# RWKV-7 layer with gated conv FFN: the Gram products of a head pair over 64 array rows each

## The chip, the cores and the metric

The kernel runs on one core of a Trainium2 chip. The metric is the device time of one execution in microseconds (us), the median of several runs.

## The reference, cut to what matters

One layer on x of 2048 tokens x 1024 channels, float32. The part concerned is the recurrence of 16 heads, each with a 64x64 state, between the projections and the output projection; a gated FFN with a causal convolution follows.

```python
def step(state, inp):                      # per head, token after token
    r_t, w_t, k_t, v_t, kk_t, a_t = inp
    sa = jnp.einsum('bhij,bhj->bhi', state, -kk_t)
    state = (state * w_t[:, :, None, :]
             + sa[..., None] * (kk_t * a_t)[:, :, None, :]
             + v_t[..., None] * k_t[:, :, None, :])
    return state, jnp.einsum('bhij,bhj->bhi', state, r_t)
...
mixed = ((y + bonus) * gate) @ w_o
x = _layer_norm(ALPHA * x + mixed, ln1_g, ln1_b)
x = _layer_norm(ALPHA * x + _conv_ffn(x, ...), ln2_g, ln2_b)
```

## The kernel before, in words

The program has four parts that overlap: projections and LoRAs (`a_nodes`), the recurrence (`s_nodes`), the output projection with its LayerNorm (`w_nodes`) and the FFN (`f_nodes`). Each adds groups of instructions to a planner (`Plan`). A group has an engine, an assumed duration, a due time and buffers of pools that it takes and gives back; the planner simulates the engines by these durations, and the order that comes out is the order in which each engine, and SP's queue of DMAs, gets its instructions. At run time an engine goes through its instructions in that order; one that waits holds all behind it.

The recurrence works on 16 tiles of 128 tokens, each of two chunks c of 64 tokens. Eight heads form a half h, so that a tile has two halves; a half has four pairs p of heads e = 0, 1. The step of 64 tokens is done as matrix products, for which the kernel needs, per head and chunk, all products between the decayed vectors: b (kk * a) and k on one side, the two vectors AR (-kk and r) on the other. These are the Gram products G. Per half:

- SP loads `l` (128 tokens x 5 x 512, 1280 KB) into the only buffer of the pool `lds`. csI (TensorE) is the running sum of the log decays, and P, Pe and Pi (ScalarE, L833) are its exponentials.
- VectorE multiplies two of the five parts of l by Pe and P (L851, L855); TensorE transposes them (tr, L878) and P (pcp, L864), ScalarE copies the former into AR.
- BKn (VectorE, L904) are b and k divided by the decay, for both chunks. b of head e lies in partitions 64e to 64e+63 and k in the other 64, so the two heads of a pair are stacked the opposite way, and each of the eight instructions takes four heads of one kind, 64x256. The last of them gives back the load buffer, and SP issues the next load.
- TensorE transposes BKn (tb, L912, rows are now channels: 64 of head 0, 64 of head 1). ScalarE copies head 0's rows into one tile and head 1's into another (BKT), whose other 64 rows were set to zero by POOL at the start. There is one such pair of tiles. G (TensorE, L744 called from f_g) is then a product over 128 rows for each head, four to a group, of which 64 rows are zeros. VectorE multiplies it by a mask (Gm, L931).

Per tile: parts of Gm go to DRAM and back transposed (NU, NUs); VectorE inverts 32 triangles of 32x32 in 31 steps of two instructions (itmp L966, XU L971); the result goes through DRAM again (XD, XT); X11 (L1000) transposes two blocks on VectorE, and two sets of small products (mp) complete the inverse of 64x64. Then the two chunks go one after the other: Z, SA, dS and Y on TensorE, copies on ScalarE (the state, later SA, into UV beside the values loaded by UV<-vc, and the decayed keys of AR into Gm), and on VectorE stmp (L1117) and state (L1122). The opposite stacking of the heads holds for UV and for all of these copies.

L744 is the helper for the products and L743 that for ScalarE's copies, so rows of these lines are told apart by the tile's name. The pools' sizes stand in `TS` (L730): one load buffer `lds`, four PSUM banks `pw` for csI, pcp, tr, tb and G, one `BKT`.

## Time and profile before

| | us |
|---|---|
| median of 3 runs | 2982.55 |
| lowest and highest | 2982.29 to 2985.43 |
| span of the profiled execution | 2981.2 |
| busy in it: TensorE | 2845.6 (95%) |
| VectorE | 2084.5 (70%) |
| ScalarE | 1740.4 (58%) |

The shares are means over parts with different limits. The projections end at about 735 us, the recurrence runs from about 690 to 1290 us, and the FFN fills TensorE to the end. A windows row gives the busy time of each engine in a stretch of 25 us, then the granted clock of TensorE (1.00 is 2.4 GHz, 0.50 is 1.2 GHz), DMA's share and GB/s. A chain row is a piece of the chain of work that ended last. Of overlapping instructions a row of the timeline shows the start of the first and the time to the end of the last.

### The profile page before, as it was taken

To read this page: it belongs to the slowest core of one execution; us is meant where nothing else is said; L and a number is where in the kernel's file an instruction comes from. 1 tells how busy PE (TensorE), PEld (TensorE's weight loads), DVE (VectorE), ACT (ScalarE), POOL (GpSimd) and SP (SyncE) were. 2 spreads that over 40 slices of the span, in tenths; PEclk is the share of its full clock that TensorE was granted. 3 is DMA by queue.
4 is the path that set the end of the run, shared out by engine and by line. 5 is a ranking of instruction groups with operands and counts; after the bars stand their busy time and mean duration, and the time that the engine had idled before them with its cause. 6 is when DMAs were issued, how large, how long until landed. Compare 5 with 4: busy or idle time off the path is not lost.

```text
span 2981.2 us, 51766 instructions
## 1 busy us (share of the span) xinstructions
PE 2845.6 (95%) x19392; PEld 2321.1 (78%) x19392; DVE 2084.5 (70%) x4288; ACT 1740.4 (58%) x4668; POOL 53.6 (2%) x96
## 2 busy tenths in 40 slices
PE   7999999998799999799999999999999999999997
PEld 5776778887677777678888887888888888888886
DVE  7888768986899999779765555474554745547454
ACT  8888557664578788878454444444444444444441
POOL 0000000001000000001100000000000000000000
PEclk9999999999899999799999999999999999999999
DMA  6346555435455565568552223242232422324222
GB/s 202 143 167 222 175 183 191 152 114 175 129 149 161 153 164 160 133 220 315 179 178 94 92 97 120 93 154 97 89 127 96 148 98 85 133 95 153 90 87 78
DMA packets 298555, 424.08 MB, mean 142 GB/s; under 512 B 153952, under 2 KB 179552, under 8 KB 294208
## 3 DMA queue, kind: packets, MB, share of 16 engines
q1 hardware_dynamic: 286976, 379.87, 39.5%
q0 software_dynamic: 11328, 40.90, 3.8%
q8 instruction: 153, 2.51, 0.4%
q14 instruction: 98, 0.80, 0.1%
HBM read 311.57 MB, written 109.12 MB: 141 GB/s over the span
## 4 chain that ended last, share of the span: by engine, by line
issue 56%; PE 20%; DVE 12%; ACT 8%; DMA 3%; POOL 1%; SPq 0%; POOLq 0%; ACTq 0%; DVEq 0%
PE ps L141 4%; PE ps L142 4%; PE ps L143 4%; DVE BKn L904 3%; ACT junk L619 3%; PE G L744 2%; DVE itmp L966 1%; DVE XU L971 1%; DVE Gm L931 1%; PE Y L744 1%; DMA l<-in 1%; ACT junk L1260 1%; PE csI L744 1%; ACT UV L743 1%; PE tb L912 1%
## 5 line engine op out<-in xcount | busy, mean ns | idle before, releaser
L143 PE MATMUL ps<-xH,wiL 128*128 128x512 f32 x1408 | 557.9, 396 | 0.5 <-DVE wiL L1571 0.3
L1571 DVE TENSOR_TENSOR wiL<-wis,wiH 128x1024 fp32r<-128x1024 f32 x176 | 215.4, 1224 | 488.5 <-ACT wiH L1432 488.5
L141 PE MATMUL ps<-xH,wiH 128*128 128x512 f32 x1408 | 556.9, 396 | 0.0
L142 PE MATMUL ps<-xL,wiH 128*128 128x512 f32 x1408 | 556.8, 395 | 0.0
L1432 ACT ACTIVATE hb<-ps 128x512 f32<-128x512 f32 x176 | 105.3, 598 | 518.9 <-PE ps L143 518.8
L141 PE MATMUL ps<-WH,xiH 128*128 128x512 f32 x768 | 307.5, 400 | 14.6 <-ACT xiH L231 9.1
L143 PEld LDWEIGHTS ps<-xH,wiL 128*128 128x128 f32 x1408 | 264.5, 188 | 65.6 <-DVE wiL L1571 2.1
L142 PEld LDWEIGHTS ps<-xL,wiH 128*128 128x128 f32 x1408 | 264.4, 188 | 63.7
L141 PEld LDWEIGHTS ps<-xH,wiH 128*128 128x128 f32 x1408 | 264.5, 188 | 62.9
L142 PE MATMUL ps<-WL,xiH 128*128 128x512 f32 x768 | 305.1, 397 | 2.0 <-DVE WL L326 2.0
L143 PE MATMUL ps<-WH,xiL 128*128 128x512 f32 x768 | 304.4, 396 | 0.0
L1599 DVE SCALAR_TENSOR_TENSOR cv<-hb,cw,cv 128x512 f32<-128x512 f32 x352 | 263.4, 748 | 20.7 <-ACT cv L1595 14.5
L142 PE MATMUL acc<-woL,aH 128*128 128x512 f32 x688 | 269.3, 391 | 1.5 <-DVE woL L1536 1.5
L143 PE MATMUL acc<-woH,aL 128*128 128x512 f32 x688 | 269.9, 392 | 0.0
L141 PE MATMUL acc<-woH,aH 128*128 128x512 f32 x688 | 268.5, 390 | 0.0
L1432 ACT ACTIVATE wiH<-wis 128x1024 fp32r<-128x1024 f32 x178 | 188.8, 1061 | 5.8 <-DMA wis<-in_w_in_dram 5.8
L141 PEld LDWEIGHTS ps<-WH,xiH 128*128 128x128 f32 x768 | 146.3, 190 | 54.4 <-ACT xiH L231 9.1
L1432 ACT ACTIVATE woH<-wos 128x512 fp32r<-128x512 f32 x172 | 108.7, 633 | 114.4 <-PE acc L143 110.1
L142 PEld LDWEIGHTS ps<-WL,xiH 128*128 128x128 f32 x768 | 146.5, 191 | 34.6 <-DVE WL L326 2.5
L143 PEld LDWEIGHTS ps<-WH,xiL 128*128 128x128 f32 x768 | 146.3, 190 | 33.5 <-DVE xiL L450 0.2
L142 PEld LDWEIGHTS acc<-woL,aH 128*128 128x128 f32 x688 | 129.2, 188 | 32.4 <-DVE woL L1536 3.1
L141 PEld LDWEIGHTS acc<-woH,aH 128*128 128x128 f32 x688 | 129.2, 188 | 29.1 <-ACT woH L1432 0.5
(243 smaller groups left out, 5351.8 us busy)
## 6 DMA issues: line engine op xcount, KB each, us to landing
wis<-in_w_in_dram SPq DMA_DIRECT2D x176, 512.0 KB
wos<-in_w_out_dram SPq DMA_DIRECT2D x172, 256.0 KB
l<-in SPq DMA_DIRECT2D x32, 1280.0 KB
xT<-in_xT_dram SPq DMA_DIRECT2D x21, 1028.0 KB
in<-kp SPq DMA_DIRECT2D x64, 256.0 KB
stg<-in_w_rkv_dram SPq DMA_DIRECT2D x48, 256.0 KB
gs<-gs SPq DMA_DIRECT2D x24, 512.0 KB
in<-kr SPq DMA_DIRECT2D x32, 256.0 KB
```

Of the source, the lines that this page charges most:

```text
L141: nc.tensor.matmul(ps, lH, rH, start=start, stop=False)
L142: nc.tensor.matmul(ps, lH, rL, start=False, stop=False)
L143: nc.tensor.matmul(ps, lL, rH, start=False, stop=stop)
L619: nc.scalar.activation(junk, Z["kr"][:, 64 * i:64 * i + 64], AF.Square, accum_out=st["ss"][:, tl, i:i + 1])
L743: CP = lambda out, in_, **kw: nc.scalar.activation(out, in_, AF.Copy, **kw)
L744: MM = lambda out, l, r, **kw: nc.tensor.matmul(out, l, r, **{**dict(start=True, stop=True), **kw}, skip_group_check=True)
L904: TT(dst[rows, :, e], pe8(l[:, 1 if part else 3], e), pe8(V[t]["Pi", h], e), op=OP.mult)
L912: nc.tensor.transpose(ps[:, p], V[t]["BKn"][:, c, hd:hd + 2].rearrange("q e i -> q (e i)"), self.ident)
L931: TT(V[t]["Gm"][:, e, c, 4 * h:4 * h + 4], V[t]["G", h, c, e], gm4, op=OP.mult)
L1432: CP = lambda out, in_, **kw: nc.scalar.activation(out, in_, AF.Copy, **kw)
L1571: TT(W["L"], W["s"], W["H"], op=OP.subtract)
L1599: STT(R[j], W["hb"][:, i:i + 512], C["cw"][:, fc, i:i + 1], R[j], op0=OP.mult, op1=OP.add)
```

## The change

Both heads of a pair now have b in partitions 0 to 63 and k in 64 to 127.

- BKn: one instruction takes eight heads of a kind and chunk, 64x512; four instead of eight per half. The planner's duration for a group goes from 0.67 to 0.6.
- BKT: tb is copied as it is, one 128x512 instead of two 64x512, into one of two buffers; the zeroed tiles are gone.
- G: a product takes 64 rows of the array, those where its head's channels are, and the two heads alternate, each into its own PSUM bank. Both banks are taken at once; the planner's duration is 1.05 for the eight, before 0.87 for each four.
- Gm, UV, X11 and the copies into them follow: the first 64 partitions are b's, the state's and SA's for both heads, the others k's and the values'. UV is loaded in two DMAs with 4 KB a row instead of four with 256 B pieces. NU reads partitions 0 to 63 for both heads. X11 is 32 partitions with both heads in them, and the mp products that read it use array rows 0 to 31 for both heads.

```diff
-              slots=dict(lds=1, pw=4, P=1, Pi=1, Pe=1, AR=4, BKn=4, Gm=4, PC=4, BKT=1, NUs=2, XU=2, XT0=1, XT1=1, X11=2, mp=1,
+              slots=dict(lds=1, pw=4, P=1, Pi=1, Pe=1, AR=4, BKn=4, Gm=4, PC=4, BKT=2, NUs=2, XU=2, XT0=1, XT1=1, X11=2, mp=1,
...
-            for i in range(sl["BKT"]):
-                BKTs.append([wkp.tile([128, 4, 128], F32, name=f"BKT{i}{e}") for e in range(2)])
...
-        def f_zero1():
-            for x in BKTs:
-                for e in range(2):
-                    nc.gpsimd.memset(x[e], 0.0)
...
                         def f_bk(t=t, h=h, c=c, part=part):
                             l = V[t][f"l{h}"]
-                            pe8 = lambda ap, e: ap[es(c)].rearrange("t (p e i) -> t p e i", e=2, i=64)[:, :, e]
-                            dst = eo(V[t]["BKn"][:, c, 8 * h:8 * h + 8])
-                            for e in range(2):
-                                rows = es(1 - e) if part else es(e)
-                                TT(dst[rows, :, e], pe8(l[:, 1 if part else 3], e), pe8(V[t]["Pi", h], e), op=OP.mult)
+                            dst = V[t]["BKn"][es(part), c, 8 * h:8 * h + 8].rearrange("t h i -> t (h i)")
+                            TT(dst, l[es(c), 1 if part else 3], V[t]["Pi", h][es(c)], op=OP.mult)
                         last = c == 1 and part == 1
-                        n_bks.append(pl.add("DVE", 0.67, hb + 1.1 + c, f_bk, [n_Pi, n_alloc, n_R, n_M] +
+                        n_bks.append(pl.add("DVE", 0.6, hb + 1.1 + c, f_bk, [n_Pi, n_alloc, n_R, n_M] +
...
                     def f_bt(t=t, h=h, c=c):
-                        x = V[t]["BKT", h, c] = BKTs[st_bkt[0] % len(BKTs)]
-                        st_bkt[0] += 1
-                        for e in range(2):
-                            CP(x[e][es(e)], V[t]["tb", h, c][es(e)])
+                        CP(tile_of(t, ("BKT", h, c), wkp, [128, 4, 128], tag="BKT", bufs=sl["BKT"]), V[t]["tb", h, c])
-                    n_bt = pl.add("ACT", 0.96, hb + 2.1 + c, f_bt, [n_tb, n_z1], take=("BKT",), give=("pw",))
+                    n_bt = pl.add("ACT", 0.6, hb + 2.1 + c, f_bt, [n_tb], take=("BKT",), give=("pw",))
...
+                    def f_g(t=t, h=h, c=c):
+                        G = [tile_of(t, ("G", h, c, e), pw, [128, 4, 128], tag="pw") for e in range(2)]
+                        for p in range(4):
+                            for e in range(2):
+                                MM(G[e][:, p], V[t]["BKT", h, c][es(e), p],
+                                   V[t]["AR"][es(e), c, 4 * h + p].rearrange("q a t -> q (a t)"))
+                    n_g = pl.add("PE", 1.05, hb + 2.2 + c, f_g, [n_bt] + evs, take=("pw", "pw"), give=("BKT",))
                     for e in range(2):
-                        def f_g(t=t, h=h, c=c, e=e):
-                            G = tile_of(t, ("G", h, c, e), pw, [128, 4, 128], tag="pw")
-                            for p in range(4):
-                                MM(G[:, p], V[t]["BKT", h, c][e][:, p],
-                                   V[t]["AR"][:, c, 4 * h + p].rearrange("q a t -> q (a t)"))
-
...
-                        n_g = pl.add("PE", 0.87, hb + 2.2 + c + 0.1 * e, f_g, [n_bt] + evs + gs, take=("pw",),
-                                     give=("BKT",) if e else ())
-                        gs.append(n_g)
...
-                        r, u = 64 * e + 32 * bk, (e * 2 + bk) * 16
+                        r, u = 32 * bk, (e * 2 + bk) * 16
...
-                    x = tile_of(t, ("X11", c), wk, [128, 8, 32], tag="X11", bufs=sl["X11"])
+                    x = tile_of(t, ("X11", c), wk, [32, 2, 8, 32], tag="X11", bufs=sl["X11"])
                     for e in range(2):
-                        nc.vector.transpose(x[es(e)], XT[es(e), :, 0:32])
+                        nc.vector.transpose(x[:, e], XT[64 * e:64 * e + 32, :, 0:32])
...
-                            MM(mp[r + 32:r + 64, p], V[t]["Gm"][r:r + 32, e, c, p, 32:64], V[t]["X11", c][r:r + 32, p],
-                               tile_position=(r, r + 32))
+                            MM(mp[r + 32:r + 64, p], V[t]["Gm"][0:32, e, c, p, 32:64], V[t]["X11", c][:, e, p],
+                               tile_position=(0, r + 32))
...
-                        CP(V[t]["Gm"][es(e), e, c, :, 0:64], V[t]["AR"][es(e), c, :, 0])
+                        CP(V[t]["Gm"][0:64, e, c, :, 0:64], V[t]["AR"][es(e), c, :, 0])
...
                 for c in range(2):
-                    src = self.S["vc", t][64 * c:64 * c + 64].rearrange("t (p e i) -> t p e i", e=2, i=64)
-                    for e in range(2):
-                        self.ld(eo(UV[:, c])[es(1 - e), :, e], src[:, :, e])
+                    self.ld(UV[64:128, c].rearrange("t h i -> t (h i)"), self.S["vc", t][64 * c:64 * c + 64])
...
-                            CP(eo(V[t]["UV"][:, c])[es(e), sl8, e], SV[i0][es(e), sl8])
+                            CP(eo(V[t]["UV"][:, c])[0:64, sl8, e], SV[i0][es(e), sl8])
...
-                            CP(eo(V[t]["UV"][:, c])[es(e), sl8, e], H["SA"][es(e), sl8])
+                            CP(eo(V[t]["UV"][:, c])[0:64, sl8, e], H["SA"][es(e), sl8])
```

The planner's result changes with it. VectorE in the first half of a tile in the steady part of the recurrence, before; l is the half's load, BKn, itmp and XU as above (itmp and XU belong to the inverse of another tile):

```order
L966 TENSOR_TENSOR itmp<-XU,NUs 128x121
L904 TENSOR_TENSOR BKn<-l_12705,Pi 64x4x64 x2
L971 TENSOR_TENSOR XU<-XU,itmp 128x11x11
L904 TENSOR_TENSOR BKn<-l_12705,Pi 64x4x64 x2
L966 TENSOR_TENSOR itmp<-XU,NUs 128x110
L904 TENSOR_TENSOR BKn<-l_12705,Pi 64x4x64 x2
L971 TENSOR_TENSOR XU<-XU,itmp 128x11x10
L904 TENSOR_TENSOR BKn<-l_12705,Pi 64x4x64 x2
L966 TENSOR_TENSOR itmp<-XU,NUs 128x108
```

The same place on VectorE now:

```order
L949 TENSOR_TENSOR itmp<-XU,NUs 128x121
L891 TENSOR_TENSOR BKn<-l_12600,Pi 64x512
L954 TENSOR_TENSOR XU<-XU,itmp 128x11x11
L891 TENSOR_TENSOR BKn<-l_12600,Pi 64x512
L949 TENSOR_TENSOR itmp<-XU,NUs 128x110
L1098 TENSOR_TENSOR stmp<-dS,state 128x512
L954 TENSOR_TENSOR XU<-XU,itmp 128x11x10
L1103 TENSOR_TENSOR state<-stmp,PC 128x512
L949 TENSOR_TENSOR itmp<-XU,NUs 128x108
L891 TENSOR_TENSOR BKn<-l_12600,Pi 64x512
L954 TENSOR_TENSOR XU<-XU,itmp 128x12x9
L891 TENSOR_TENSOR BKn<-l_12600,Pi 64x512
```

stmp and state, which stood behind the half's last BKn, now stand between its two chunks.

TensorE at the second half of a tile in the steady part, before (csI to tb are the half's, SA, dS and Y another tile's chunk step):

```order
L744 MATMUL csI<-l_9669,c_triI 128x512
L744 MATMUL G<-AR,BKT_7382 128x128 x4
L744 MATMUL SA<-Zs,XT_7829 64x64 x16
L864 MATMUL pcp<-ident,P 128x128 x4
L878 MATMUL tr<-ident,l_9669 128x128 x8
L744 MATMUL dS<-UV,BKn 64x64 x16
L912 MATMUL tb<-ident,BKn 128x128 x8
L744 MATMUL G<-AR,BKT_7381 128x128 x4
L744 MATMUL Y_9767<-UV,Gm 64x64 x16
L744 MATMUL G<-AR,BKT_7382 128x128 x4
```

TensorE at the second half of a tile now:

```order
L744 MATMUL G<-AR,BKT 128x128 x8
L744 MATMUL SA<-Zs,XT_7822 64x64 x16
L744 MATMUL csI<-l_10745,c_triI 128x512
L744 MATMUL dS<-UV,BKn 64x64 x16
L854 MATMUL pcp<-ident,P 128x128 x4
L868 MATMUL tr<-ident,l_10745 128x128 x8
L899 MATMUL tb<-ident,BKn 128x128 x8
L744 MATMUL G<-AR,BKT 128x128 x16
```

G now stands in eights and sixteens and SA ahead of csI, and dS has moved from behind tr to directly behind csI.

## Rows read from the trace of the kernel before

**Rows 1.** Table of windows: PE, PEld, DVE, ACT, POOL busy us, clock, DMA

```profile
750.00:775.00 25.00, 18.42 (x95) 15.35 (x95) 20.56 (x71) 9.38 (x19) 0.00 (x0) 0.73 0.49 146
...
800.00:825.00 25.00, 19.96 (x310) 16.45 (x311) 23.50 (x81) 14.87 (x29) 0.54 (x1) 1.00 0.58 169
...
1050.00:1075.00 25.00, 22.42 (x425) 19.35 (x420) 24.18 (x82) 20.02 (x42) 0.00 (x0) 1.00 0.48 127
1075.00:1100.00 25.00, 23.92 (x472) 20.35 (x471) 23.98 (x82) 21.95 (x44) 0.53 (x1) 1.00 0.61 168
```

**Rows 2.** List of waits, 875 to 1200 us: total, times, longest

```profile
PE csI L744 <- DMA l<-in: 1.3, 3, 0.6
...
DVE l L855 <- ACT P L833: 0.6, 1, 0.6
```

**Rows 3.** Groups of VectorE by form, 875 to 1200 us

```profile
L904 DVE TENSOR_TENSOR BKn<-l,Pi 64x256 f32<-64x256 f32 x166 | 68.6, 418 | 3.1 <-ACT Pi L833 0.3
...
L855 DVE TENSOR_TENSOR l<-l,P 128x512 f32<-128x512 f32 x21 | 14.4, 684 | 0.6 <-ACT P L833 0.6
```

**Rows 4.** Chain of waits, 719 to 727 us: start, us, what

```profile
719.34 6.20 DMA l<-in
725.58 1.14 PE csI L744 x2
```

**Rows 5.** Timeline of TensorE, 750 to 757 us: start, us, what

```profile
750.00 5.46 PE L744 MATMUL G<-AR,BKT 128*128 128x128 f32 x32
755.30 1.02 PE L744 MATMUL csI<-l,c_triI 128*128 128x512 f32 x2
```

**Rows 6.** Timeline of VectorE, second half of a tile, 1099 to 1104 us

```profile
1099.85 2.50 DVE L904 TENSOR_TENSOR BKn<-l,Pi 64x256 f32<-64x256 f32 x6
1102.38 0.27 DVE L971 TENSOR_TENSOR XU<-XU,itmp 128x110 f32<-128x110 f32 x1
1102.68 0.86 DVE L904 TENSOR_TENSOR BKn<-l,Pi 64x256 f32<-64x256 f32 x2
1103.57 0.29 DVE L966 TENSOR_TENSOR itmp<-XU,NUs 128x126 f32<-128x126 f32 x1
```

**Rows 7.** Timeline of VectorE, 1066 to 1068 us

```profile
1066.22 0.68 DVE L855 TENSOR_TENSOR l<-l,P 128x512 f32<-128x512 f32 x1
1066.82 0.68 DVE L931 TENSOR_TENSOR Gm<-G,c_gmask 128x512 f32<-128x512 f32 x1
```

**Rows 8.** Timeline of TensorE, 1064 to 1067 us

```profile
1064.67 1.05 PE L744 MATMUL G<-AR,BKT 128*128 128x128 f32 x8
1065.65 1.15 PE L744 MATMUL SA<-Zs,XT 64*64 64x64 f32 x32
1066.73 0.66 PE L864 MATMUL pcp<-ident,P 128*128 128x128 f32 x4
```

**Rows 9.** List of waits, 690 to 875 us

```profile
ACT BKT L743 <- PE G L744: 17.0, 10, 2.8
...
DVE Gm L931 <- PE G L744: 14.1, 13, 3.6
```

**Rows 10.** Groups of ScalarE by form, 875 to 1200 us

```profile
L743 ACT ACTIVATE BKT<-tb 64x512 f32<-64x512 f32 x81 | 47.9, 592 | 11.8 <-PE tb L912 10.3
...
L743 ACT ACTIVATE Zs<-Z 128x512 f32<-128x512 f32 x18 | 10.7, 597 | 0.2
```

**Rows 11.** Timeline of SP's queue, 1011 to 1014 us

```profile
1011.27 2.59 SPq L124 DMA_DIRECT2D UV<-vc  x4
```

**Rows 12.** Chain of waits, at the last tile

```profile
1210.40 3.52 DMA NU<-Gm
```

**Rows 13.** Chain of waits, a load of the steady part

```profile
1008.51 8.39 DMA l<-in
```

**Rows 14.** Chain of waits, G at the low and at the high clock

```profile
765.70 3.43 PE G L744 x16
...
1058.67 1.98 PE G L744 x16
```

More of the change, by code (lines that the diff above doesn't have):

```diff
@@ L746, in s_nodes @@
         es = lambda e: slice(64 * e, 64 * e + 64)
-        st_bkt = [0]
         eo = lambda tl: tl.rearrange("q (p e) i -> q p e i", e=2)
@@ L800, in s_nodes @@
         cst = wk = ch2 = sm = pm = pc = None
-        chs, XTs, BKTs, SV, ZS, SW, V = [None] * sl["AR"], [], [], {}, {}, {}, {}
+        chs, XTs, SV, ZS, SW, V = [None] * sl["AR"], [], {}, {}, {}, {}
         n_o1 = pl.add("-", 0, 0, f_open1, [n_1])
         n_o2 = pl.add("-", 0, 0, f_open2, [n_o1, n_2])
-        n_z1 = pl.add("POOL", 2.0, -9.0, f_zero1, [n_o1], lat=0.2)
         n_z2 = pl.add("POOL", 4.0, -9.0, f_zero2, [n_o2], lat=0.2)
@@ L915, in f_bt @@
                     def f_bt(t=t, h=h, c=c):
-                        x = V[t]["BKT", h, c] = BKTs[st_bkt[0] % len(BKTs)]
-                        st_bkt[0] += 1
-                        for e in range(2):
-                            CP(x[e][es(e)], V[t]["tb", h, c][es(e)])
+                        CP(tile_of(t, ("BKT", h, c), wkp, [128, 4, 128], tag="BKT", bufs=sl["BKT"]), V[t]["tb", h, c])
                     n_tb = pl.add("PE", 0.44, hb + 2.0 + c, f_tb, n_bks[2 * c:2 * c + 2], take=("pw",))
-                    n_bt = pl.add("ACT", 0.96, hb + 2.1 + c, f_bt, [n_tb, n_z1], take=("BKT",), give=("pw",))
-                    gs = []
-                    for e in range(2):
-                        def f_g(t=t, h=h, c=c, e=e):
-                            G = tile_of(t, ("G", h, c, e), pw, [128, 4, 128], tag="pw")
-                            for p in range(4):
-                                MM(G[:, p], V[t]["BKT", h, c][e][:, p],
-                                   V[t]["AR"][:, c, 4 * h + p].rearrange("q a t -> q (a t)"))
+                    n_bt = pl.add("ACT", 0.6, hb + 2.1 + c, f_bt, [n_tb], take=("BKT",), give=("pw",))
[6 more added lines that the diff above has]
+                    n_g = pl.add("PE", 1.05, hb + 2.2 + c, f_g, [n_bt] + evs, take=("pw", "pw"), give=("BKT",))
+                    for e in range(2):
                         def f_gm(t=t, h=h, c=c, e=e):
                             TT(V[t]["Gm"][:, e, c, 4 * h:4 * h + 4], V[t]["G", h, c, e], gm4, op=OP.mult)
-                        n_g = pl.add("PE", 0.87, hb + 2.2 + c + 0.1 * e, f_g, [n_bt] + evs + gs, take=("pw",),
-                                     give=("BKT",) if e else ())
-                        gs.append(n_g)
                         grams.append(pl.add("DVE", 0.6, hb + 2.3 + c + 0.1 * e, f_gm, [n_g], give=("pw",)))
```

## The prediction

> **What bounds the kernel now.** I read the table of windows first. In the steady part of the recurrence (about 800 to 1201 us) VectorE is busy 24.18 and 23.98 of 25 us, while TensorE has 22.42 and 23.92 and ScalarE 20.02 and 21.95 [rows 1]. VectorE is full there: in the list of waits of 875 to 1200 us the longest wait of VectorE for another engine is 0.6 us, and TensorE waited for the load of the recurrence's inputs 1.3 us in all [rows 2]. So a time taken off VectorE is a time taken off that stretch, until something else is late. The stretch's pace comes from the grouped instructions: 166 BKn of 8 per half tile are 20.75 halves in 325 us, 15.66 us a half and 31.3 us a tile [rows 3].
>
> Before 800 us it is another limit. At 750 to 775 us no engine is full (TensorE 18.42, VectorE 20.56) and the granted clock is 0.73 [rows 1]. The chain there runs in a ring: load, csI, P, the decayed l, BKn, and the next load, since there is one load buffer and the last BKn gives it back. One such ring shows in the chain of waits: the load takes 6.20 us and csI starts 0.04 us behind it [rows 4]. TensorE goes its queue in order, so csI can also stand behind the G products: 32 records of G take 5.46 us at this clock and csI starts right behind them [rows 5]. After 1201 us the last tiles' latency counts, then the FFN, whose work is untouched.
>
> **The sum.** It is made against the profiled span of 2981.2 us; the median of the runs, 2982.55 us, lies 1.35 us above it, and I carry that difference over.
>
> *BKn, 8 of 64x256 to 4 of 64x512 per half.* The timeline shows 8 BKn with one XU between them from 1099.85 to 1103.57, 3.72 us; the XU takes 0.30 of it (1102.38 to 1102.68), so 3.42 us, 0.43 each, which is the record's 418 ns and 0.01 [rows 3, 6]. No 64x512 of VectorE is in the trace. The nearest row is the 128x512 product l·P, with the same number of elements in a partition: a record of 684 ns [rows 3], whose successor starts 0.60 us after it [rows 7]. The new one costs 0.60 us if its successor starts as early, and 0.70 if it starts after the record's end, as behind the BKn of now. Four are 2.40 to 2.80 us, so a half saves 0.62 to 1.02 us. The operands still alternate between the lower and upper 64 partitions, as now, so I stay near 0.70 and take 0.65.
>
> The Trainium skill, page "VectorE: DVE Perf Modes", section "Two Vector instructions with no wait between them", says that an instruction whose inputs or output begin in another quadrant than those of the one ahead starts only when all earlier ones have finished. The rows agree: 0.60 us between two 128x512 that start alike, 0.43 us for a 418 ns record that doesn't. By that rule alone three or four of each four new BKn cost 0.70, and the sum below would be 2961 rather than 2960.
>
> The last 24 of the 32 halves lie in the full stretch (400 us at 15.66, less the cut one): 24 x 0.65 = 15.6 us. Seven halves lie on the ring of 700 to 800 us, where the last BKn releases the load: 7 x 0.65 = 4.6 us. The first half lies beside the projections.
>
> *G over 64 rows.* Each product is two records. Four G products with 128 columns take 0.98 us (1064.67 to 1065.65), 0.245 each; SA, 16 products of 64 columns that alternate between two quarters of the array, takes 1.08 (to 1066.73), 0.0675 each [rows 8]. At G's rate 64 columns would take 0.122; so SA runs 1.8 abreast. A tile has 32 G products, 7.8 us; at 1.8 they are 4.3. TensorE's load per tile, 46.34/50 x 31.3 = 29.0 us [rows 1], falls to 25.5. In the steady stretch that is hidden behind VectorE and counts nothing. On the ring it counts where csI or the mask Gm wait for G: VectorE waited 14.1 us for G in 690 to 875 us, ScalarE's BKT copy 17.0 us for G, for want of a second BKT [rows 9]. Both buffers and products now come sooner, but csI is then held by the load (6.20 us from the last BKn is about where csI starts now). The gain is between 0 and 14.1 us; I take 0.4 us a half, 3 us, because the ring row shows only 0.04 us between load and csI.
>
> *BKT, one copy for two.* Two of 592 ns become one of 128x512, like Zs at 597 ns [rows 10]: 64 x 0.59 = 38 us off ScalarE, hidden, as VectorE hardly waits for ScalarE [rows 2]. The zeroing on POOL was off the path.
>
> *Moved rows.* The copies of decayed keys, state and SA into rows 0 to 63 keep their shapes; X11 becomes 32x256 and keeps its elements in a partition. The mp products of both heads share 32 array rows now in other columns; dS and Z share rows in this way already and are as fast as SA, so nothing. UV goes in two issues instead of the four that take 2.59 us on SP's queue [rows 11], ahead of NU and of the next load: at best 1.3 us earlier for what is queued behind, on a stretch where loads are seldom late. NU reads 64 partitions for both heads. This is covered while VectorE has other inverses to do; at the end, where the last NU stands on the chain with 3.52 us [rows 12], it costs between 0 and once more that. I take 1 us.
>
> The Trainium skill, page "SBUF — State Buffer", section "Door 1: The DMA port swizzle", speaks against this part: partitions of one half reach only 8 of 16 ports. By it the tail's NU could double, 3.5 us, and the sum would be 2963. No row here shows such a load.
>
> Sum: 2982.5 - 15.6 - 4.6 - 3 + 1 = **2960 us**.
>
> **Rivals.** (a) *More comes back.* New BKn overlap fully (0.60): 31 halves x 1.02 = 31.6 us, and the ring gives 7 us: 2944 us. For it: the 128x512 pitch [rows 7]. Against: today's BKn don't overlap [rows 6].
>
> (b) *The row halves don't run side by side.* No product over 64 rows and 128 columns is in the trace; only quarters and column halves are. Then TensorE keeps 29.0 us for a tile that should take 30.0, 97%, where its fullest window now has 23.92 of 25 [rows 1], 96%. About half of the steady gain is lost, and the 3 us: 2982.5 - 7.8 - 4.6 = 2970 us. The Trainium skill, page "TensorEngine Tiling (Array Packing)", section "Key Properties", says that a change of tiling mode drains TensorE, which would add to this case; in the trace G and SA follow one another at their usual pitch [rows 8].
>
> (c) *A wait takes the freed place.* The planner now puts dS behind csI, and stmp, which reads dS, between the two BKn pairs of a half. A load that lands late, as that of 1008.51 with 8.39 us against 6.20 [rows 4, 13], then holds csI, dS, stmp, and behind stmp the two BKn that free the load buffer. If this costs 1.3 us a tile the steady gain is gone and the ring's is partly: 2978 to 2982 us. Against: csI waited for loads only 1.3 us in 325 [rows 2], and two UV issues burden the queues less.
>
> (d) *Slower: TensorE's clock falls in the steady stretch.* With 25.5 us of work in 30.0 TensorE has idle time that it hasn't now. 16 records of G take 3.43 us at the low level (1.2 GHz) and 1.98 at the high one (2.4 GHz) [rows 14], 1.73 times as long. A tile of 25.5 us lasts over 31.3 once a third of its work runs low: 25.5 x (1 + 0.73 s) > 31.3 from s = 0.31. At s = 0.5 it is 34.8, 3.5 us more over 12.8 tiles (400 us), 45 us; less the ring's 7, 3020 us. For it: at 750 to 775 us the granted clock was 0.73 with 18.42 busy. Against: at 800 to 825 us it stayed 1.00 with 19.96 of 25, 80%, less than the 85% to come [rows 1]. The Trainium skill, page "TensorE: Matmul & The Clock Gate", section "Why this matters for your kernels", warns of idle gaps between bursts, which is this rival's reason.
>
> **How the numbers follow.** Chances: forecast 0.57 (2950 to 2968), (a) 0.10, (b) 0.16, (c) 0.08, (d) 0.09. The forecast's own range comes from 0.62 to 1.02 us a half, 0 to 7 on the ring and 0 to 3.5 at the tail. The range of 8 in 10 takes in (a) and (b): 2944 to 2976 us. Faster by over 0.2% (6 us, about what a measurement of this kernel can tell from no change) are forecast, (a) and (b): 0.83; same is (c), 0.08; slower is (d), 0.09.
>
> **What would show it.** Right: 4 BKn of some 684 ns a half and a tile of about 30 us between 875 and 1150 us with VectorE still at 96%; G records 16 in about 1.1 us; a BKT copy of 0.6 us; granted clock 1.00. Wrong: VectorE below 93% there, with stmp waiting for dS or Gm for G (c, b); G 16 in 2 us (b); granted clock under 1.00 in the steady windows (d); ring halves at 15 us as now; a tail longer than now between the last Gm and the first FFN product, for which I have 1 us.

## The result and the profile after

The changed kernel takes 2998.67 us (median; 2995.38 to 3005.86) beside 2982.92 us for the kernel before on the same chip: ratio 1.0052, 95% interval 1.0036 to 1.0068. It is slower, where 2960 us was forecast. The profiled span is 2993.6 us, 12.4 more than before. By the end of each half's last BKn and of the last Y:

| stretch | before | after | difference |
|---|---|---|---|
| to the end of the 2nd half | 719.3 | 716.6 | -2.7 |
| 3rd to 10th half (the ring) | 129.9 | 128.0 | -1.9 |
| 11th to 28th half (nine steady tiles) | 286.2 | 296.7 | **+10.5** |
| 29th to 32nd half | 65.6 | 66.9 | +1.3 |
| last BKn to last Y | 83.4 | 88.3 | **+4.9** |
| last Y to the first FFN product | 206.3 | 206.7 | +0.4 |

The table of windows after, columns as in [rows 1]:

```profile
750.00:775.00 25.00, 15.87 (x103) 10.86 (x104) 22.17 (x68) 8.44 (x18) 0.00 (x0) 0.77 0.56 154
...
800.00:825.00 25.00, 18.15 (x328) 13.90 (x322) 21.37 (x58) 14.23 (x29) 0.54 (x1) 0.86 0.60 149
...
1050.00:1075.00 25.00, 23.40 (x484) 19.12 (x480) 21.91 (x77) 19.70 (x41) 0.53 (x1) 0.93 0.52 141
1075.00:1100.00 25.00, 21.67 (x464) 18.30 (x466) 21.85 (x63) 19.10 (x40) 0.53 (x1) 0.93 0.63 173
```

VectorE has fallen from 24 to under 22 of 25 us, and the granted clock from 1.00 to 0.86 to 0.93. VectorE is no longer full, and its list of waits after, 875 to 1200 us, where before its longest was 0.6 [rows 2], says for whom it waits:

```profile
DVE l L845 <- ACT P L823: 9.0, 10, 2.3
DVE Gm L917 <- PE G L744: 8.2, 12, 1.2
DVE l L841 <- ACT Pe L823: 3.4, 9, 0.7
DVE BKn L891 <- ACT Pi L823: 2.6, 8, 0.7
DVE stmp L1098 <- PE dS L744: 1.7, 3, 1.1
```

What the change was to make cheaper is cheaper. Groups after, 875 to 1200 us, answering [rows 3, 10]:

```profile
L891 DVE TENSOR_TENSOR BKn<-l,Pi 64x512 f32<-64x512 f32 x79 | 54.1, 685 | 4.4 <-ACT Pi L823 2.6
L744 PE MATMUL G<-AR,BKT 64*128 64x128 f32 x640 | 53.5, 324 | 1.1 <-ACT BKT L743 1.1
...
L743 ACT ACTIVATE BKT<-tb 128x512 f32<-128x512 f32 x40 | 23.5, 598 | 29.2 <-PE tb L899 29.1
```

BKn of a half after, on VectorE's timeline: from 1040.69 to 1043.86 with one XU between, 3.17 us where [rows 6] had 3.72:

```profile
1040.69 2.10 DVE L891 TENSOR_TENSOR BKn<-l,Pi 64x512 f32<-64x512 f32 x3
1042.82 0.29 DVE L954 TENSOR_TENSOR XU<-XU,itmp 128x126 f32<-128x126 f32 x1
1043.14 0.69 DVE L891 TENSOR_TENSOR BKn<-l,Pi 64x512 f32<-64x512 f32 x1
1043.86 0.28 DVE L949 TENSOR_TENSOR itmp<-XU,NUs 128x120 f32<-128x120 f32 x1
```

The timeline of TensorE after shows G at both levels of the clock, and what the steady stretch lost:

```profile
1031.10 1.16 PE L744 MATMUL G<-AR,BKT 64*128 64x128 f32 x16
1032.19 0.65 PE L899 MATMUL tb<-ident,BKn 128*128 128x128 f32 x4
...
1042.21 0.63 PE L899 MATMUL tb<-ident,BKn 128*128 128x128 f32 x4 [0.86 <-ACT AR L743]
1043.97 1.08 PE L899 MATMUL tb<-ident,BKn 128*128 128x128 f32 x4 [1.14 <-DVE BKn L891]
1044.99 3.79 PE L744 MATMUL G<-AR,BKT 64*128 64x128 f32 x32
1048.70 1.06 PE L744 MATMUL mp<-X,Gm 32*32 32x32 f32 x32
1049.69 1.98 PE L744 MATMUL Y<-UV,Gm 128*64 128x64 f32 x32
1051.60 1.06 PE L744 MATMUL mp<-XT,FT 32*32 32x32 f32 x32
1052.59 1.50 PE L744 MATMUL Z<-UV,Gm 128*64 128x64 f32 x32
1054.02 1.12 PE L744 MATMUL csI<-l,c_triI 128*128 128x512 f32 x2
```

At the high level eight G products take 1.09 us (1031.10 to 1032.19), against 0.98 for four [rows 8]: 1.8 abreast. At 1042 us TensorE waits 0.86 us for AR's copy, then 1.14 us for BKn. The clock of 1043 to 1053 us, a windows row of after, is 0.51, the low level:

```profile
1043.00:1053.00 10.00, 9.03 (x140) 8.26 (x142) 8.20 (x21) 5.36 (x10) 0.00 (x0) 0.51 0.60 168
```

The 16 G products of two groups (32 records) take 3.79 us there, and what stands ahead of csI is slow too: Y 1.98 us, against 1.15 us at the high level (880.18 us), and two mp of 1.06, against 0.69. Five tiles earlier the same place had two pauses as long and no fall of the clock: G took 2.06 us. So such pauses do not bring the low level each time. Timeline of TensorE and a windows row, after:

```profile
875.17 0.63 PE L899 MATMUL tb<-ident,BKn 128*128 128x128 f32 x4 [0.87 <-ACT AR L743]
876.92 0.63 PE L899 MATMUL tb<-ident,BKn 128*128 128x128 f32 x4 [1.12 <-DVE BKn L891]
877.48 2.06 PE L744 MATMUL G<-AR,BKT 64*128 64x128 f32 x32
...
875.00:900.00 25.00, 22.33 (x510) 18.96 (x510) 23.46 (x76) 19.76 (x40) 0.53 (x1) 1.00 0.66 188
```

In the slow tile csI is late, P on ScalarE waits for it behind Zs, and VectorE stands at Gm and at the decayed product. Timeline of VectorE, after:

```profile
1047.10 1.29 DVE L917 TENSOR_TENSOR Gm<-G,c_gmask 128x512 f32<-128x512 f32 x2 [1.02 <-PE G L744]
...
1055.96 0.69 DVE L845 TENSOR_TENSOR l<-l,P 128x512 f32<-128x512 f32 x1 [1.58 <-ACT P L823]
```

Timeline of ScalarE, after:

```profile
1054.14 0.60 ACT L743 ACTIVATE Zs<-Z 128x512 f32<-128x512 f32 x1 [0.26 <-PE Z L744]
1055.24 0.69 ACT L823 ACTIVATE P<-csI,c_cols 128x512 f32<-128x512 f32 x1 [0.51 <-PE csI L744]
```

So VectorE waits for results that come late, while TensorE itself has time to spare. In this tile both the low clock and the products that stand ahead of csI in the queue make csI late. Which of them costs the time, the experiments tell.

### The profile page after: what moved, and what is told of

It is laid out like the page before. It is cut to its first block, busy times and chain, and to the rows that moved or that the text cites. A ratio compares the mean times of both kernels' runs of the same rounds, so it can differ in the third digit from the quotient of the medians.

```text
span 2993.6 us, 51468 instructions
## 1 busy us (share of the span) xinstructions
PE 2828.6 (94%) x19392; PEld 2290.7 (77%) x19392; DVE 2066.9 (69%) x4160; ACT 1702.8 (57%) x4604; POOL 52.6 (2%) x94
## 4 chain that ended last, share of the span: by engine, by line
issue 55%; PE 20%; DVE 10%; ACT 8%; DMA 5%; POOL 1%; SPq 0%; POOLq 0%; ACTq 0%; DVEq 0%
PE ps L141 4%; PE ps L142 4%; PE ps L143 4%; ACT junk L619 3%; DVE BKn L891 2%; DMA l<-in 1%; DVE itmp L949 1%; DVE XU L954 1%; PE G L744 1%; DVE Gm L917 1%; DMA NU<-Gm 1%; DMA NUs<-NU 1%; DMA stg<-in_w_rkv_dram 1%; PE csI L744 1%; ACT UV L743 1%
## 5 line engine op out<-in xcount | busy, mean ns | idle before, releaser
L143 PEld LDWEIGHTS ps<-xH,wiL 128*128 128x128 f32 x1408 | 264.6, 188 | 65.6 <-DVE wiL L1552 2.1
```

The lines of the kernel that those rows point to most:

```text
L143: nc.tensor.matmul(ps, lL, rH, start=False, stop=stop)
```

## The experiments

All kernels compute the whole layer. In the table the nine steady tiles are counted from VectorE's records in each trace: gaps over 60 ns are its wait, the rest its work; the clock is the mean granted one there. The ratio is to the kernel before in the same comparison.

| kernel | median us | ratio, interval | tile | work | wait | clock |
|---|---|---|---|---|---|---|
| before | 2982.92 | | 31.80 | 31.65 | 0.14 | 0.994 |
| after | 2998.67 | 1.0052 (1.0036 to 1.0068) | 32.96 | 30.37 | 2.59 | 0.908 |
| e1_fill | 2998.35 | 1.0045 (1.0029 to 1.0061) | 32.24 | 30.33 | 1.91 | 0.988 |
| e2_gpad | 2974.47 | 0.9959 (0.9944 to 0.9974) | 31.23 | 31.01 | 0.22 | 1.000 |
| e3_bkn8 | 3017.59 | 1.0112 (1.0089 to 1.0135) | 34.30 | 30.88 | 3.42 | 0.867 |
| e5_gseq | 3010.31 | 1.0080 (1.0052 to 1.0108) | 33.06 | 31.16 | 1.90 | 0.937 |
| e6_g174 | 2984.33 | 1.0006 (0.9994 to 1.0018) | 32.96 | 31.31 | 1.65 | 0.942 |
| e7_g130 | 2983.93 | 1.0001 (0.9987 to 1.0014) | 31.31 | 29.96 | 1.35 | 0.952 |
| e8_b060 | 3020.55 | 1.0120 (1.0103 to 1.0137) | 35.45 | 32.59 | 2.86 | 0.936 |
| e9_g174_fill | 2981.19 | 0.9991 (0.9981 to 1.0001) | 31.29 | 31.19 | 0.10 | 1.000 |
| e10_g130_fill | 2989.27 | 1.0008 (0.9995 to 1.0021) | 31.39 | 30.14 | 1.25 | 1.000 |
| e13_csi | 3005.89 | 1.0067 (1.0047 to 1.0087) | 33.01 | 30.32 | 2.69 | 0.925 |
| e14_csi_fill | 3010.00 | 1.0087 (1.0072 to 1.0101) | 33.43 | 30.35 | 3.09 | 0.960 |
| e15_regular | 3024.18 | 1.0131 (1.0117 to 1.0144) | 35.08 | 30.62 | 4.46 | 0.908 |
| e16_irregular | 3013.69 | 1.0113 (1.0096 to 1.0131) | 33.70 | 31.03 | 2.67 | 0.944 |
| e17_regular_fill | 3023.90 | 1.0137 (1.0121 to 1.0152) | 34.76 | 30.53 | 4.23 | 0.984 |
| e18_pz | 3000.15 | 1.0042 (1.0028 to 1.0055) | 32.80 | 30.24 | 2.56 | 0.914 |
| e19_pz_fill | 3004.84 | 1.0057 (1.0041 to 1.0073) | 32.52 | 30.31 | 2.22 | 1.000 |
| e20_reg_pz_fill | 3023.27 | 1.0126 (1.0112 to 1.0141) | 34.61 | 30.45 | 4.16 | 0.984 |
| e21_before_zp | 2994.05 | 1.0027 (1.0016 to 1.0038) | 32.77 | 31.74 | 1.02 | 0.991 |

**The clock alone.** Four constant products ahead of each tb fill the pause.

```diff
                     def f_tb(t=t, h=h, c=c):
                         ps = tile_of(t, ("tb", h, c), pw, [128, 4, 128], tag="pw")
+                        for p in range(4):
+                            MM(ps[:, p], self.ident, gmask)
```

> The changed kernel with four products of constants (128x128, written to the bank that the transposes tb then overwrite) ahead of each tb group; nothing else differs, and the order of all other instructions is that of the changed kernel. They fill the time in which TensorE waits for BKn. Theory C (the clock): the changed kernel loses because TensorE stands idle there, its granted clock falls to 1.2 GHz, and the G, Y, Z and csI behind run slow, so that P and VectorE's l x P come late. Then the granted clock is 1.00 or nearly in the windows of 875 to 1200 us and the time is about 2962 us (2955 to 2975). Theory O (the order): the planner's new order loses by itself. Then the clock is 1.00 and the time stays at 2988 to 3000 us. Theory N (NU reads one half of the partitions, its transfer is late): also 2988 or more.

The clock came back and the time did not. A windows row and a wait of e1_fill:

```profile
975.00:1000.00 25.00, 21.30 (x457) 17.69 (x458) 20.45 (x70) 17.29 (x35) 0.00 (x0) 1.00 0.56 151
```

```profile
DVE l L845 <- ACT P L823: 9.4, 8, 3.0
```

At 1.00 VectorE still has only 20.45 of 25 us in this window, the lowest of 875 to 1100 us (the other eight, all at 1.00, have 22.27 to 24.02), and it waits for P as in the changed kernel. The nine steady tiles did become 0.72 us shorter each. Behind them it was taken back: the 29th to 32nd half take 70.9 us (66.9 in the changed kernel), and from the last BKn to the last Y it is 90.9 us (88.3). The clock is not the whole cause.

**Parts of the change.** e2_gpad keeps the stacking and the wide BKn, but has G over 128 rows with zeroed halves as before; e5_gseq has G over 64 rows in two groups, one head after the other; e3_bkn8 has eight BKn of 64x256 again.

The core of e2_gpad:

```diff
-                                MM(G[e][:, p], V[t]["BKT", h, c][es(e), p],
-                                   V[t]["AR"][es(e), c, 4 * h + p].rearrange("q a t -> q (a t)"))
-                    n_g = pl.add("PE", 1.05, hb + 2.2 + c, f_g, [n_bt] + evs, take=("pw", "pw"), give=("BKT",))
...
+                                MM(G[:, p], V[t]["BKT", h, c][e][:, p],
+                                   V[t]["AR"][:, c, 4 * h + p].rearrange("q a t -> q (a t)"))
...
+                        n_g = pl.add("PE", 0.87, hb + 2.2 + c + 0.1 * e, f_g, [n_bt] + evs + gs, take=("pw",),
```

of e5_gseq, whose groups are the same but for the 64 rows:

```diff
+                                MM(G[:, p], V[t]["BKT", h, c][es(e), p],
+                                   V[t]["AR"][es(e), c, 4 * h + p].rearrange("q a t -> q (a t)"))
```

and of e3_bkn8:

```diff
-                            TT(dst, l[es(c), 1 if part else 3], V[t]["Pi", h][es(c)], op=OP.mult)
+                            for e in range(2):
+                                TT(dst[es(part), :, e], pe8(l[:, 1 if part else 3], e), pe8(V[t]["Pi", h], e), op=OP.mult)
```

> The changed kernel with G as before: products over 128 rows with zeros in the other head's, two groups of four with the planner's durations of before, two 64x512 copies into one pair of zeroed BKT tiles. BKn in four 64x512, the alike stacking, UV, NU and X11 are those of the changed kernel. Theory C: TensorE has as much to do as before, the clock is 1.00 at 875 to 1200 us, and what the four BKn save counts: 2960 to 2970 us. Theory N: 2985 us or more, since NU reads as in the changed kernel. Theory O says nothing of it, since the order is another again.

> The changed kernel with G over 64 rows, but in two groups, one for each head, so that four products on the same array rows follow one another; planner's durations of before for G, one 128x512 BKT copy into two buffers. Products on the same rows can't run abreast, so 8 records take about 1.0 us as before and TensorE has the work of before. Theory C: clock 1.00 at 875 to 1200 us and 2956 to 2968 us, as e2_gpad or a little less. Theory N: 2985 or more. If 64-row products are faster even one after another (G of 8 records in 0.6 us): the clock falls as in the changed kernel and the time is 2985 to 3000.

> The changed kernel with BKn in eight instructions of 64x256 per half (planner's duration of before), the stacking alike for both heads; G over 64 rows as changed. If the 20 us that the four BKn save on VectorE are on the path in the changed kernel: 3010 to 3022 us. If VectorE is no limit there and waits for csI whatever it does (C): 2995 to 3008 us, with the clock below 0.95 at 875 to 1200 us.

e2_gpad beats both kernels, though it stays short of its 2960 to 2970 us: VectorE is full and the clock whole (a windows row of e2_gpad):

```profile
1050.00:1075.00 25.00, 23.79 (x470) 20.24 (x468) 24.02 (x73) 19.96 (x40) 0.53 (x1) 1.00 0.55 143
```

So the stacking and the wide BKn can be had without the loss, which came in with the new G and what the planner made of it. e5_gseq, whose G is not abreast (625 records in 83.2 us of busy time, where the changed kernel has 640 in 53.5), was to be fast (2956 to 2968 us) and is slower still. Its instructions are nearly e2_gpad's; its order is another. e3_bkn8 also has its own order, so its 18 us over the changed kernel are not the price of BKn alone: work is 0.5 us a tile more and wait 0.8. Its group of BKn shows where the gain of BKn comes from (875 to 1200 us, e3_bkn8):

```profile
L893 DVE TENSOR_TENSOR BKn<-l,Pi 64x256 f32<-64x256 f32 x152 | 57.3, 415 | 2.4 <-ACT Pi L823 0.7
```

An instruction is as long as before, but with the alike stacking the sixteen of a tile overlap: 0.38 us of busy time each, against 0.41 [rows 3]. About half of what the change saves on BKn comes from the stacking, not from the wider instructions.

**The order alone.** The planner is told another duration of G; the instructions stay the same. (e7_g130 has one BKT buffer as well.)

e6_g174 (1.3 in e7_g130), in the changed kernel:

```diff
-                    n_g = pl.add("PE", 1.05, hb + 2.2 + c, f_g, [n_bt] + evs, take=("pw", "pw"), give=("BKT",))
+                    n_g = pl.add("PE", 1.74, hb + 2.2 + c, f_g, [n_bt] + evs, take=("pw", "pw"), give=("BKT",))
```

e8_b060, in the kernel before:

```diff
-                        n_g = pl.add("PE", 0.87, hb + 2.2 + c + 0.1 * e, f_g, [n_bt] + evs + gs, take=("pw",),
+                        n_g = pl.add("PE", 0.6, hb + 2.2 + c + 0.1 * e, f_g, [n_bt] + evs + gs, take=("pw",),
```

> The changed kernel with one number of the planner changed: the G group's assumed duration is 1.74 (that of the two groups of before) instead of 1.05. The instructions are the same, only their order on the engines differs. With 1.05 the planned intervals between the tiles' inverses scatter from 26.2 to 32.1, with 1.74 they are 29.8 from tile to tile, the same order in each tile, as before the change. Theory R (the order is what loses): the irregular order holds together only at the planner's durations, and real waits break it. Then this kernel is at 2958 to 2972 us, and VectorE is busy 95% in 875 to 1200 us. Theory C (the clock alone) or a loss in the instructions themselves (side-by-side products, NU from one half): 2988 to 3002 us.

> As the run with 1.74, but with 1.30 for the G group and one BKT buffer; the planned interval is 28.4 from tile to tile, and regular. Theory R, regularity alone: 2955 to 2972 us. If what counts is how much slack the planner leaves and not that the order repeats: the tighter plan loses, 2980 to 3000 us. Theory C: 2985 or more, with a granted clock below 0.95 at 875 to 1200 us.

> The kernel before with one number of the planner changed: each G group's assumed duration is 0.60 instead of 0.87. Its instructions are those of the kernel before; the planned intervals between tiles now scatter from 26.3 to 33.2. Theory R: slower than before, by 10 to 30 us (2992 to 3012). If the loss comes from the changed instructions and not from the order: 2978 to 2988, as before.

This is the clearest result. The same instructions in another order are 14 us faster in the changed kernel (the two ratios' intervals don't meet), and 36 us slower in the kernel before, where VectorE then waits for G and P as in the changed kernel. The 14 us show in the medians only: the profiled execution of e6_g174 is its slowest, and its tiles are as long as the changed kernel's. And they are the loss alone: e6_g174 and e7_g130 are level with the kernel before, above the 2955 to 2972 us that theory R gave them. From the list of waits of e8_b060:

```profile
DVE Gm L931 <- PE G L744: 13.2, 26, 2.1
...
DVE l L855 <- ACT P L833: 6.8, 5, 2.9
```

**Order and clock together.** e6_g174 and e7_g130 with the four products ahead of tb and three ahead of csI.

```diff
+                    for p in range(3):
+                        MM(ps[:, 128 * p:128 * p + 128], self.ident, gmask)
                     MM(ps, tri, V[t][f"l{h}"][:, 4])
```

> The run with the G group planned at 1.74 (regular order), and products of constants in TensorE's two waiting places: four ahead of each tb group and three ahead of each csI, into the banks that these then overwrite. In the profile of the run without them the granted clock was 0.80 to 0.93 in six of the thirteen windows of 875 to 1200 us, and in those VectorE was busy 20.65 to 22.49 of 25 us, where at 1.00 it was 24.0. Theory R+C (first the order, then the clock): clock 1.00 in those windows, VectorE at 24 of 25, and 2960 to 2972 us, with a narrower spread from run to run. If the clock is only a sign of the waits: the time stays at 2979 to 2993 us at clock 1.00, as the first run with such products did in the irregular order.

> The run with the G group planned at 1.30 and one BKT buffer, with the same products of constants ahead of tb and csI. Theory R+C: 2955 to 2970 us at clock 1.00 from 875 to 1200 us. If the tight plan leaves TensorE no room for seven more products a chunk or the clock is only a sign: 2978 to 2995 us.

With e6_g174's order and the products the clock is 1.00 and the wait falls from 1.65 to 0.10 us a tile, measured from e6_g174's slowest execution (2993.61 us). A gain in time is not shown: the medians are 2984.33 and 2981.19 us, and the intervals of their ratios overlap. Both expectations, 2960 to 2972 and 2955 to 2970 us, were missed: with e7_g130's tighter order 1.25 us of wait stay at a clock of 1.00, and the median does not gain. A windows row of e9_g174_fill:

```profile
1050.00:1075.00 25.00, 24.79 (x446) 21.45 (x446) 23.99 (x75) 17.16 (x37) 0.33 (x1) 1.00 0.54 154
```

So with VectorE full and the clock whole the kernel is only level with the one before. Its nine steady tiles take 4.6 us less than before's, where 1.3 us a tile would be 11.7, and from the last BKn to the last Y it needs 7.8 us more.

**Which property of the order?** e13_csi puts csI ahead of the Z that it stood behind, nine times; e14_csi_fill adds e1_fill's products. e15_regular and e16_irregular tell the planner longer VectorE durations, so that its tiles come every 30.4 us all alike, or every 30.3 us on average but unlike; e17_regular_fill adds the products. e18_pz moves csI and, on ScalarE, P and Pe ahead of Zs, as before has them; e19_pz_fill adds the products, e20_reg_pz_fill has these moves in e17_regular_fill; e21_before_zp makes the opposite moves in the kernel before.

The move on TensorE (e13_csi, e18_pz), and that on ScalarE (e18_pz), as rows of the order:

```diff
 MATMUL mp<-XT,FT 32x32 x16
+MATMUL csI<-l,c_triI 128x512
 MATMUL Z<-UV,Gm 64x64 x16
-MATMUL csI<-l,c_triI 128x512
 MATMUL mp<-X,Gm 32x32 x16
```

```diff
+ACTIVATE P<-csI,c_cols 128x512
+ACTIVATE Pe<-csI,c_cols 128x512
 ACTIVATE Zs<-Z 128x512
-ACTIVATE P<-csI,c_cols 128x512
-ACTIVATE FT<-mp 32x256 x2
-ACTIVATE Pe<-csI,c_cols 128x512
+ACTIVATE Pi<-csI,c_cols 128x512
+ACTIVATE FT<-mp 32x256 x2
 ACTIVATE UV<-SA 64x8x64 x2
-ACTIVATE Pi<-csI,c_cols 128x512
```

The durations of e15_regular; e16_irregular has 0.70 for BKn, 0.65 for Gm and 0.65 for l*P and l*Pe (0.60 before):

```diff
-                        n_bks.append(pl.add("DVE", 0.6, hb + 1.1 + c, f_bk, [n_Pi, n_alloc, n_R, n_M] +
+                        n_bks.append(pl.add("DVE", 0.7, hb + 1.1 + c, f_bk, [n_Pi, n_alloc, n_R, n_M] +
...
-                        grams.append(pl.add("DVE", 0.6, hb + 2.3 + c + 0.1 * e, f_gm, [n_g], give=("pw",)))
+                        grams.append(pl.add("DVE", 0.68, hb + 2.3 + c + 0.1 * e, f_gm, [n_g], give=("pw",)))
...
-                n = pl.add("DVE", 0.67, mc, f_x11, [n_xt], take=("X11",))
+                n = pl.add("DVE", 0.9, mc, f_x11, [n_xt], take=("X11",))
```

> The changed kernel with one thing moved: where TensorE's queue has csI directly behind a Z, csI is put ahead of that Z. This happens nine times in the recurrence, once per tile in its steady part; nothing else moves on any engine. Theory L (csI stands behind Z, and Z waits for copies or runs at the low clock, so P comes late): in 875 to 1200 us VectorE's wait of 9.0 us for P falls below 3 us, those for Pe and Pi fall with it, VectorE stands above 22.5 of 25 us in most windows, and the median falls from 2998.67 to 2986 to 2992 us. Theory R (the whole order counts, not this one place): VectorE's waits shift to Gm or stmp and the median stays at 2996 to 3001 us. Against both: if the load lands too late, csI now holds Z and the state's chain, and it is slower, above 3001 us.

> The same move of csI with four constant products put ahead of each tb, which kept TensorE's granted clock at 1.00 in most steady windows of the changed kernel. If order and clock are the two parts of the loss, and csI behind Z is the order's part, this one has VectorE at 23.5 to 24 of 25 us in the steady windows and a median of 2976 to 2986 us. If the order counts as a whole, it stays where the products alone were, 2995 to 3000 us. If the clock is all that the move leaves, it is below the run without the products by 5 us or more.

> The changed kernel's instructions in another order: the planner keeps its G duration of 1.05 and is told longer VectorE durations, BKn 0.70, Gm 0.68, X11 0.90 in place of 0.60, 0.60, 0.67. Its tiles then come every 30.4 us, each planned alike, where the changed kernel's plan has 26.2 to 32.1 us with a mean of 29.1; csI still stands behind Z. Theory P (regular tiles): VectorE's wait in nine steady tiles falls from 2.6 us a tile to under 0.7 us if TensorE's clock holds, to 1.0 to 1.7 us if the clock stays near 0.94, and the median is 2974 to 2988 us. Theory Z (csI behind Z, or one such place): as the changed kernel, 2995 to 3001 us.

> Again the changed kernel's instructions, the planner now told BKn 0.70, Gm 0.65 and the two decayed products 0.65: its tiles come every 30.3 us on average, as in the run with all tiles alike, but at 27.9 to 33.6 us. If the mean slack in the plan decides, it is as fast as that run within 5 us and VectorE waits as little. If the tiles have to be alike, VectorE waits 1.9 us a tile or more, as in the changed kernel, and the median is 2992 to 3004 us.

> The run with tiles of 30.4 us all alike, with four constant products ahead of each tb and three ahead of each csI. If the clock is the second part of the loss, TensorE's clock stands at 1.00 in the steady windows, VectorE waits under 0.4 us a tile there, and the median is 2972 to 2982 us, at or below the run without the products; if what the clock gives is taken back by the recurrence's end, as it was with the other regular order, the nine steady tiles are shorter by 3 us or more and the median moves by less than that.

> The changed kernel with csI ahead of Z on TensorE, as in the run that moved csI alone, and now also the exponentials of that csI on ScalarE put as the kernel before has them: P and Pe ahead of Zs and Pi directly behind it, where the changed kernel has Zs, P, FT, Pe, UV from SA, Pi. Eight or nine places of each, nothing else moves. Theory Q (the load's chain csI, P, Pe, Pi stands behind the state's chain Z, Zs, SA in two queues, so both have to be mended): first products on VectorE start later than P's end again, VectorE's waits for P, Pe and Pi together fall from 15.0 us in 875 to 1200 us to under 6 us, the wait per steady tile from 2.6 to 0.6 to 1.5 us, and the median to 2984 to 2992 us. Theory W (the order as a whole): waits move to Gm or stmp, median 2996 to 3008 us.

> The same moves with four constant products ahead of each tb and three ahead of each csI. Theory Q with the clock as the second part: granted clock 1.00 in the steady windows, a wait of under 0.8 us per steady tile, a median of 2974 to 2986 us. Theory W: 2996 to 3012 us.

> The order with all tiles alike and the constant products, with the same moves of csI and of P, Pe and Pi. Theory Q: its wait of 4.2 us per steady tile falls below 2 us and its median from 3023.90 to 2985 to 3005 us. Theory W: above 3012 us.

> The kernel before with the opposite moves and nothing else: Z ahead of csI on TensorE and Zs ahead of P and Pe on ScalarE, at ten places. Theory Q: VectorE begins to wait for P, 0.5 to 2 us per steady tile, and the kernel takes 2988 to 3005 us. Theory W: no change, 2980 to 2987 us.

Every theory of a single property fell. With csI ahead of Z, it took 2.87 us from csI's start to P's in first halves (1.55 in the changed kernel, 1.07 before): P stood behind Zs on ScalarE. e15_regular, planned with tiles all alike, is the slowest of all, while e6_g174's plan, alike from tile to tile too, is among the good ones. With both queues mended the waits for P, Pe and Pi fell from 15.0 to 5.7 us, but the state's chain is now late. From the list of waits of e18_pz:

```profile
DVE stmp L1116 <- PE dS L761: 13.2, 7, 3.9
DVE Gm L935 <- PE G L761: 5.1, 7, 1.2
DVE l L863 <- ACT P L840: 4.6, 7, 2.1
```

Two chains, load to BKn and Z to state, meet in TensorE's, ScalarE's and VectorE's queues, and in these orders a place given to one is taken from the other: the wait per tile is 2.56 us after the moves, 2.59 ahead of them. Spoiling the good order in the same ten places does cost, 1.0 us a tile and some 8 us in all (a wait of e21_before_zp):

```profile
DVE l L895 <- ACT P L872: 6.7, 9, 0.8
```

So these places matter but don't suffice. That the loss against the kernel before is the order's is shown. Which property of an order makes it good is open; neither the mean of the planned tiles nor their likeness is it.

## Why the prediction was wrong

- *BKn, 0.65 us a half.* Held, as the cost of the instructions: 3.17 us against 3.72 in the rows shown, and 1.28 us less work in a steady tile, against 1.3. In e2_gpad, whose VectorE is full as before, only 0.64 us a tile came back: its BKn take 5.60 us a tile where before's take 6.84, but more itmp are followed at once by their own XU, 18 a tile against 15. At 0.13 us each (last section) these three are an estimated 0.4 of the missing 0.6 us; the rest is open. A full engine gained less than the sum of the cheaper instructions.
- *G 1.8 abreast.* Held, at 1.09 us for eight. The Trainium skill, "TensorEngine Tiling (Array Packing)", section "Key Properties", has a drain at a change of mode. The trace agrees, and it is short: in the kernel before, the next record starts 0.11 us behind the last one of G where it is csI, over 128 rows too, and 0.205 us where it is SA, so the "usual pitch" of [rows 8] had a change in it; G over 64 rows is followed by tb after 0.203 us. At some 0.1 us a change it leaves 1.8 abreast. Rival (b) is out.
- *"In the steady stretch that is hidden behind VectorE and counts nothing."* **This is the step that failed**, and it failed twice. The planner lays out every queue by the durations it is told, so a shorter G changed the place of csI, P, stmp, G and Y on all engines; the order rows ahead of the prediction showed it, and I took each moved row for a matter of one wait. e6_g174, where only the planned G is longer, and e8_b060, where only it is shorter, show what the order is worth: 14 and 36 us. And time freed on TensorE became pauses ahead of tb, with the mean clock of the steady tiles at 0.908 where it was 0.994, and at 0.51 in the tile shown, just where Gm and csI wait. This second part made the steady tiles longer (0.72 us each, by e1_fill); that it costs time in the whole is not shown. Of the 38.7 us between forecast and result the order accounts for some 14; the rest is gain that stayed out, and the best kernel, e2_gpad, brought 11 us of it.
- *Rival (c)*, 2978 to 2982 us, was right that a wait takes the freed place, and wrong on its chain and its price. It had late loads hold csI, dS and stmp; after, in 875 to 1200 us, stmp waits for dS only 1.7 us, csI for DMAs 2.9 us, and the long waits are for P and G. It stopped at the loss of the gain; the wait is 2.45 us a tile more than before, 1.9 times the gain.
- *Rival (d)* was priced as throughput: TensorE over 31.3 us a tile from s = 0.31. TensorE never became full (18.15 to 23.40 of 25 us in the windows shown); what the low clock cost came as latency. The pace of 31.3 us a tile, counted from the BKn of a window that cuts tiles, was 0.5 short as well: nine whole tiles before take 31.80 each. "Against: at 800 to 825 us it stayed 1.00" took the clock of one order for that of another: the same window now shows 0.86. The Trainium skill, "TensorE: Matmul & The Clock Gate", section "Why this matters for your kernels", warns of idle gaps between bursts, but of longer ones than the 0.86 and 1.14 us that stand at the fall to 0.51 here.
- *The ring, 4.6 and 3 us.* 1.9 us came, and 2.7 ahead of it: VectorE's wait for G fell from 14.1 [rows 9] to 5.9 us, but csI waited 14.7 us for the load. The term was too large by some 3 us. e2_gpad, with the new BKn and the G of before, has a ring of 123.2 us, 6.7 less than before, so the shortfall is not BKn's.
- *The tail, 1 us for NU.* NU itself takes 3.77 us on the chain of waits after, against 3.52 [rows 12]. The Trainium skill, "SBUF — State Buffer", section "Door 1: The DMA port swizzle", has one half of the partitions reach only half of the ports; the doubling that the prediction worked out from it is not seen. But the tail is 4.9 us longer. Chain of waits after:

```profile
1218.28 3.77 DMA NU<-Gm
...
1239.94 7.15 DMA XT<-XD
```

The last X wait for XT, timeline of VectorE after:

```profile
1241.42 0.43 DVE L983 STREAM_TRANSPOSE X<-XT 32x256 f32<-32x256 f32 x1 [0.44 <-DMA XT<-XD]
1244.45 0.43 DVE L983 STREAM_TRANSPOSE X<-XT 32x256 f32<-32x256 f32 x1 [1.28 <-DMA XT<-XD]
...
1247.12 0.43 DVE L983 STREAM_TRANSPOSE X<-XT 32x256 f32<-32x256 f32 x1 [2.24 <-DMA XT<-XD]
```

That is 3.96 us of waits, 0.90 in the kernel before (timeline of VectorE, before):

```profile
1229.97 0.44 DVE L1000 STREAM_TRANSPOSE X<-XT 64x256 f32<-64x256 f32 x1 [0.90 <-DMA XT<-XD]
```

Why XT lands late there (loads of wos and wE stand beside it in SP's queue) was not tried. Another order alone can lengthen this stretch: in e8_b060, with the instructions of before, it takes 88.6 us (88.3 in the changed kernel). The tail also takes back what e9_g174_fill gains: its last BKn ends 9.4 us earlier than before's, its last Y 1.6.

## What to carry to other kernels

Where a planner sets in-order queues from durations, a cheaper instruction on an engine that is not the bound is no free change: its new planned duration re-lays every queue. Change the number alone and the instructions alone, each by itself, before believing either, and read a moved row as a place in a chain that crosses engines. Keep the order with the gain: e2_gpad, with the wide BKn and the old G, is the best version found.

## What was not expected of the hardware

- Two short pauses of TensorE, 0.86 and 1.14 us, came with 10 us at the low level (0.51 from 1043 to 1053 us) though TensorE was busy 9.03 of these 10 us. Pauses of 0.87 and 1.12 us at 875 to 877 us did not. With constant products in these places the clock stood at 1.00 in most steady windows (e1_fill).
- On VectorE an itmp that is followed by its own XU costs more than its record of 0.29 us: the XU starts 0.33 us after it. With another operation behind it, the next starts 0.20 us after it. Timeline of VectorE, e9_g174_fill:

```profile
1012.10 0.29 DVE L953 TENSOR_TENSOR itmp<-XU,NUs 128x128 f32<-128x128 f32 x1
1012.43 0.29 DVE L958 TENSOR_TENSOR XU<-XU,itmp 128x128 f32<-128x128 f32 x1
...
1015.21 0.28 DVE L953 TENSOR_TENSOR itmp<-XU,NUs 128x120 f32<-128x120 f32 x1
1015.41 0.69 DVE L843 TENSOR_TENSOR l<-l,Pe 128x512 f32<-128x512 f32 x1
```
